# mLSTM keys laid out by token: transposing DMAs over halves of words in place of products with the identity

## The chip, the cores and the metric

The kernel runs on 1 core of one Trainium2 chip. The metric is device time in microseconds (us); the kernel before takes 910.33 us, the median of three runs (909.4 to 910.87). Lower is better.

## The reference, cut to what matters

One layer of a hybrid decoder on 1024 prompt tokens and on 8 single tokens with a saved state. One large input projection feeds two branches, a gated linear recurrence (RG-LRU) and an mLSTM with 4 heads of 256 features; the gated results of both go through an output projection and a norm. The change touches the mLSTM alone, which runs over chunks of 128 tokens:

```python
u = hn @ w_in                       # (1024 tokens) x (1024 -> 7168 + 8 columns)
xa, za, uq, uk, uv, uo, zb, ui, uf = split(u)
k = uk.reshape(B, S, H_B, DK) * DK ** -0.5

def mlstm_chunk(carry, inp):        # q, k, v: (B, L=128, H=4, 256)
    C, n, m = carry
    ...
    P = w * einsum('bthk,bshk->bhts', q, k)
    num = (einsum('bhts,bshv->bthv', P, v)
           + ginter[..., None] * einsum('bthk,bhkv->bthv', q, C))
    den = sum(P, -1) + ginter * einsum('bthk,bhk->bht', q, n)
    h = num / maximum(abs(den), exp(-m_t))
    C_new = carry_scale * C + einsum('bhs,bshk,bshv->bhkv', decay, k, v)
    n_new = carry_scale * n + einsum('bhs,bshk->bhk', decay, k)
    return (C_new, n_new, mL), h
```

(`ginter`, `carry_scale` and `decay` are broadcast as the letters say.) Two sums use the keys in two layouts. The scores (`P`) sum over the 256 features, so TensorE wants features on its partitions. The memory (`C_new`) sums over the 128 tokens, so there the keys are wanted with tokens on the partitions.

## The kernel before, in words

Everything runs on one core, in one program without loops at run time. The Tile framework's scheduler fixes the order of each engine's instructions; each engine and each DMA queue then works strictly in order. Loads (`ld`) stand in the queue of SyncE (SP), stores (`stq`) in that of GpSimd (POOL).

**Projections.** The input projection is done in 14 units of two column pairs each (`UNITS`, in the order `v0v1 x0y0 q0k0 x1y1 q1k1 x2y2 v2v3 q2k2 x3y3 q3k3 o0o1 o2o3 z0z1 z2z3`). A unit is 14 pieces: the seven products of a Strassen scheme, each for two halves. All large products are made of three: each operand is split into a high part and a low rest (`split`, L70 to L74: a cast on ScalarE, a subtraction on VectorE), and `mm3` (L64 to L68) multiplies high by high, high by low and low by high. A unit's weights come by two loads of L258 into `raw`. ScalarE and VectorE bring the results from PSUM into staging tiles (`stg`, made by `sg`, 2 KB per partition each); there are seven of them (`NSTG`), used in turn by all that asks for one. From a staging tile POOL's queue stores to scratch memory in DRAM: queries and keys of head h to `d_qk[h]` ([4, 128, 1024]: two blocks of query features, two of key features, features on partitions), values to `d_v[h]`, gates to others.

**Work in between.** After each piece `pop_bg` (L730) takes one step from each of three lists of small work: `bg`, `rgq` (the RG-LRU, with loads of `xs` and `zsr` at L764, L766 and L770 and its gates' weights at L798) and, at the pieces in `DEC`, `dcq` (the 8 single tokens). What is put on the list `late` runs one round later.

**The mLSTM.** There are 32 items, n = 4 x chunk + head. The first four run during the last unit (`m_first`), the other 28 in the final loop, where the products of the output projection (`fill`: `mm3` with `ps_o<-wo,mh`) are laid between their steps. For one item:

- `m_load(n)` loads queries and keys (`qk`, 128 x 4 x 128) and values (`vt`, 128 x 256), each into one of two buffers, two items ahead. `w_load` brings the row of decays `W`.
- `m_k(n)` makes the weights `We` (L1213), and splits queries and memory (`qh`/`ql`, `Ch`/`Cl`).
- `m_a(n)` makes, in one PSUM bank `s`, the scores (two products in full float32, which the profile counts as four instructions at L1232) and beside them the keys with tokens on partitions: `TE.transpose` of the two key blocks, products with the identity `idF` (L1234). ScalarE then makes the scaled keys `kh` from that bank (L1240), VectorE their rest `kl` (L1242) and the weighted scores `pf` (L1241); values and weighted scores are split (`vh`/`vl`, `ph`/`pl`).
- `m_b(n)` makes query times memory (`qp`, six products), which ScalarE scales (L1288), keys times values (`kv`, six), scores times values (`tr`, three), and updates the memory `Cf`.
- Later steps normalise (`so`, L1313), transpose the head's output (L1339) and split it into `mh`/`ml`, the operands of the output projection.

Of the kernel before, what the change touches and what calls it, by code (L numbers as in the profile page):

```python
# [9 lines left out]
F32 = mybir.dt.float32  # L10
F32R = mybir.dt.float32r
BF16 = mybir.dt.bfloat16
AF = mybir.ActivationFunctionType
ALU = mybir.AluOpType
PSUM = bass.MemoryType.PSUM
# [28 lines left out]
UNITS = "v0v1 x0y0 q0k0 x1y1 q1k1 x2y2 v2v3 q2k2 x3y3 q3k3 o0o1 o2o3 z0z1 z2z3".split()  # L44
NWS, NSTG, LEAD = 6, 7, 2
DEC = 4, 5, 7, 9, 11
RQ = [Q_P1, Q_P2, Q_P5, Q_P6, Q_P7, Q_P4, Q_P3]
NR, NZ = 28, 4

# [2 lines left out]
def hymba_kernel(  # L52
# [118 lines left out]
    d_gd = dram.tile([NB, 8], F32, name="d_gd")  # L171
    d_dv = [dram.tile([NB, 256], F32, name=f"d_dv{h}") for h in range(NH)]
    d_qk = [dram.tile([4, P, T], F32, name=f"d_qk{h}") for h in range(NH)]
    d_v = [dram.tile([T, 256], F32, name=f"d_v{h}") for h in range(NH)]
    d_so = [dram.tile([T, 256], F32, name=f"d_so{h}") for h in range(NH)]
    d_zs = dram.tile([KC, P, T], F32, name="d_zs")
# [226 lines left out]
    grow = [sg([1, HT], f"grow{half}") for half in range(2)]  # L403
    for half in range(2):
        A.dma_start(grow[half], g_norm[:, half * HT:(half + 1) * HT])
    warm = const([P, 1], "warm")
    A.activation(warm, ones[:, 0:1], AF.Sqrt)
    es_f = ExitStack()
    fp = es_f.enter_context(tc.tile_pool(name="f_start", bufs=1))
# [315 lines left out]
        V.tensor_scalar(em_t, em_t, 1e-15, None, op0=ALU.max)  # L725
        V.tensor_scalar(de_t, de_t, 1.0 / 16.0, None, op0=ALU.mult)

    bg, rgq, dcq = deque(), deque(), deque()

    def pop_bg(n=1, rg=1, dc=1):  # L730
        run_late()
        for q, m in ((bg, n), (rgq, rg), (dcq, dc)):
            for _ in range(m):
                if q:
                    q.popleft()()
# [216 lines left out]

    ds_ = {}

    def dec_rows(half):

        pvd = ps("s", [NB, 512])
        for m in range(4):
            TE.transpose(pvd[:, m * P:(m + 1) * P], dv[:, 4 * half + m, :], idF)
        vr = sg([NB, 512], "vr")  # L960
        V.tensor_copy(vr, pvd)
        for h in range(2):
            stq(d_dv[2 * half + h], vr[:, h * 256:(h + 1) * 256])
# [112 lines left out]
    def decode_outputs():  # L1076
# [45 lines left out]
            V.tensor_tensor(v4(nn, kb), v4(nq, kb), bh(dGI), op=ALU.mult)  # L1122
            V.tensor_tensor(v4(kwn, kb), v4(dk, kb), bh(dW), op=ALU.mult)
        V.tensor_tensor(nn, nn, kwn, op=ALU.add)
        nrow = mx["pn"].tile([64, 512], F32, tag="nrow", name="nrow")
        for half in range(2):
            g = slice(32 * half, 32 * half + NB)
            pn = ps("s", [NB, 512])
# [4 lines left out]

    es_m, es_n, es_t = ExitStack(), ExitStack(), ExitStack()
    mx = {}

    def m_open1():

        fpr["es"].close()
        mx["p"] = mp = es_m.enter_context(tc.tile_pool(name="f_m1", bufs=1, reuse_waits="tile"))
        mx["Cf"] = [mp.tile([P, 2, 258], F32, tag=f"Cf{h}", name=f"Cf{h}") for h in range(NH)]
        mx["v"] = vhl = [mp.tile([P, 258], F32R, tag=f"v{n}", name=f"v{n}") for n in "hl"]
        mx["pn"] = es_n.enter_context(tc.tile_pool(name="f_mn", bufs=1, reuse_waits="tile"))
        V.memset(vhl[0][:, 256:257].bitcast(F32), 1.0)
        V.memset(vhl[0][:, 257:258].bitcast(F32), 0.0)
        V.memset(vhl[1][:, 256:258].bitcast(F32), 0.0)
        w_load(0)
        m_load(0)  # L1150
        m_load(1)
        so_load(0)
        so_load(1)

    def m_open2():

        es_n.close()
        es_d.close()
        pt = es_t.enter_context(tc.tile_pool(name="f_mt", bufs=1, reuse_waits="tile"))
        w_fetch(0, 1, pt.tile([P, 4, HT], F32, tag="wc01", name="wc01"))  # L1160
        m_load(4)
        m_load(5)
# [9 lines left out]
    def m_load(n):  # L1172
        if n >= 4 * NCH:
            return
        c, h = n // 4, n % 4
        ts_ = slice(c * L, (c + 1) * L)
        w_load(n + 1)
        qk = mx["p"].tile([P, 4, L], F32, tag="qk", name="qk", bufs=2)
        ld(qk, d_qk[h][:, :, ts_].rearrange("m p t -> p m t"))
        vt = mx["p"].tile([P, 256], F32, tag="vt", name="vt", bufs=2)  # L1180
        ld(vt, d_v[h][ts_, :])
        it[n] = {"qk": qk, "vt": vt}

    Ws = {}

# [39 lines left out]
    def m_a(n):  # L1225
        c, h = n // 4, n % 4
        d = it[n]
        sk = ps("s", [P, 512])
        S, kn = sk[:, 0:128], sk[:, 256:512]
        qk = d["qk"]  # L1230
        for kb in range(2):
            TE.matmul(S, qk[:, 2 + kb, :], qk[:, kb, :], start=kb == 0, stop=kb == 1)  # L1232
        for kb in range(2):
            TE.transpose(kn[:, kb * P:(kb + 1) * P], qk[:, 2 + kb, :], idF)  # L1234
        pf = mx["p"].tile([P, L], F32, tag="pf", name="pf")
        ph = mx["p"].tile([P, L], F32R, tag="ph", name="ph")
        pl = mx["p"].tile([P, L], F32R, tag="pl", name="pl")
        kh = mx["p"].tile([P, 256], F32R, tag="kh", name="kh")
        kl = mx["p"].tile([P, 256], F32R, tag="kl", name="kl")
        A.mul(kh, kn, de_t[:, c, h:h + 1])  # L1240
        V.scalar_tensor_tensor(pf, S, 1.0 / 16.0, d["W"], op0=ALU.mult, op1=ALU.mult)  # L1241
        V.scalar_tensor_tensor(kl, kn, de_t[:, c, h:h + 1], kh.bitcast(F32), op0=ALU.mult, op1=ALU.subtract)  # L1242
        split(mx["v"][0][:, 0:256], mx["v"][1][:, 0:256], d["vt"])
        split(ph, pl, pf)
        d.update(ph=ph, pl=pl, kh=kh, kl=kl)

    def m_kv(n, tags):

# [310 lines left out]
            wo_split(m14=3, m15=12)  # L1559

    def fms():
        return mx["p2"].tile([P, 4], F32, tag="fms", name="fms", bufs=2)

    tails, stored = [], []

# [78 lines left out]
        stq(p_n[0, 0].rearrange("h (kb p) -> (h kb) p", p=P), rows)  # L1644

    def last_tile():
        ms = mx["p2"].tile([P, 6], F32, tag="ms7", name="ms7")
        y = [sg([P, HT], f"y{n}") for n in range(2)]
        yg = [sg([P, HT], f"yg{n}") for n in range(2)]
        for n in range(2):  # L1650
# [83 lines left out]
    for u in range(1, len(units)):  # L1734
        roles_on()
        for n, (q, s) in enumerate(PIECES):
            if n in PREP:
                preps(7 * (u - 1) + PREP.index(n) + 1 + LEAD)
            product(u, q, s)
            pop_bg(2 if u == 1 or u == last_u else 1, 1, part % 14 in DEC)  # L1740
            part += 1
            if u == last_u and n in DUE:
                wo_due(DUE.index(n))
            if n == 13:
                for kind, j in units[u]:
                    if kind == "x":
                        rg_unit(j)
                for half in range(2):
                    if u == max(unit_of["v", 2 * half], unit_of["v", 2 * half + 1], 1):
                        bg.append(lambda half=half: dec_rows(half))  # L1750
                for h in range(NH):
                    if done_h[h] == u:
                        bg.append(lambda h=h: decode_queue(h))
                if u == last_u - 1:
                    dgen = decode_outputs()

                    def step():
                        next(dgen, None)
                        run_late()
                    state["out"] = [step] * 5 + [m_open2]  # L1760
            if n % 2 and not state["m"] and u > max(done_h) and not (bg or rgq or dcq or late):
                m_start()
            if u == last_u and n == 1:
                if not state["m"]:
                    while bg or rgq or dcq or late:
                        pop_bg()
                    m_start()
                bg.extend(state["out"])
# [11 lines left out]
    for n in range(4, N):  # L1780
# [7 lines left out]
        if n == 6:  # L1788
            mx["gf"] = gf = [sg([P, HT], f"gf{m}") for m in range(2)]
            for m in range(2):  # L1790
                stq(gf[m], g_final[m * HT:(m + 1) * HT].partition_broadcast(P))
        m_load(n + 2)
        if h == 3 or n == 4:
            z_load(c if h == 3 else 0)
        if h == 0:
# [78 lines left out]
```

## Time and profile before

| | before |
|---|---|
| median of three runs | 910.33 us (909.4 to 910.87) |
| profiled execution, its own time | 909.62 us |
| its span in the profile | 907.8 us |
| ScalarE, DMA moved | busy 586.1 us (65%), 167.76 MB |
| HBM read, written | 108.00 MB, 62.92 MB |
| chain that ended last, largest lines | TensorE's `ps_o` L66 6%, L68 6%, L67 6%; `ps_s` L1232 1%; `ps_s` L1234 1% |

The profile is one execution. Busy time of an engine is the sum over its instructions; PE is TensorE's multiplying, PEld its loading of weights, which runs beside it; DVE is VectorE, ACT ScalarE, POOL GpSimd, and SPq the queue of loads. A row of the order of time has the start in the span (us), the duration (us), the engine, the line, the operation and the tiles, output left of `<-`, with buffer numbers left out. A row of the groups has the count after x, the busy time (us), the mean (ns), and the idle time of that engine just before with what ended it. A row of the waits has engine, tile and line of who waits, then for whom, then the summed wait, how many, and the longest.

### The profile page before, as it was taken

To read this page: it belongs to the slowest core of one execution; us is meant where nothing else is said; L and a number is where in the kernel's file an instruction comes from. 1 tells how busy PE (TensorE), PEld (TensorE's weight loads), DVE (VectorE), ACT (ScalarE), POOL (GpSimd) and SP (SyncE) were. 2 spreads that over 40 slices of the span, in tenths; PEclk is the share of its full clock that TensorE was granted. 3 is DMA by queue.
4 is the path that set the end of the run, shared out by engine and by line. 5 is a ranking of instruction groups with operands and counts; after the bars stand their busy time and mean duration, and the time that the engine had idled before them with its cause. 6 is when DMAs were issued, how large, how long until landed. Compare 5 with 4: busy or idle time off the path is not lost. (4 is left out here: it accounts for less than half of the span.)

```text
span 907.8 us, 16671 instructions
## 1 busy us (share of the span) xinstructions
PE 895.5 (99%) x5889; PEld 764.4 (84%) x5889; DVE 740.4 (82%) x1528; ACT 586.1 (65%) x1086; POOL 194.9 (21%) x322
## 2 busy tenths in 40 slices
PE   8999999999999999999999999999999999999996
PEld 6997778887888998888889998887788888888885
DVE  6974779869689978798999877679998779888973
ACT  7663446767667776576768775547787568556652
POOL 1111113012222222323333244010111111111120
PEclk9999999999999999999999999999999999999999
DMA  6412457347556557657585555536689889856531
GB/s 200 152 62 92 140 155 262 112 154 233 192 188 217 179 176 235 202 158 243 188 272 191 193 179 189 170 124 226 202 228 256 203 224 287 216 144 178 178 123 70
DMA packets 127037, 167.76 MB, mean 185 GB/s; under 512 B 17212, under 2 KB 94084, under 8 KB 126946
## 3 DMA queue, kind: packets, MB, share of 16 engines
q1 hardware_dynamic: 105334, 103.68, 37.1%
q0 software_dynamic: 21616, 63.02, 21.6%
q8 instruction: 46, 0.75, 0.4%
q14 instruction: 37, 0.30, 0.1%
q10 hardware_dynamic: 4, 0.00, 0.0%
HBM read 108.00 MB, written 62.92 MB: 188 GB/s over the span
## 5 line engine op out<-in xcount | busy, mean ns | idle before, releaser
L72 ACT CAST wh<-raw 128x1024 fp32r<-128x1024 f32 x91 | 95.4, 1049 | 72.8 <-DVE raw L299 21.2
L73 DVE TENSOR_TENSOR wl<-raw,wh 128x1024 fp32r<-128x1024 f32 x91 | 111.1, 1221 | 36.7 <-ACT wh L72 21.4
L66 PE MATMUL ps_X<-cb_hi,wh 128*128 128x512 f32 x320 | 126.6, 396 | 0.0
L68 PE MATMUL ps_X<-cb_hi,wl 128*128 128x512 f32 x320 | 125.4, 392 | 0.0
L67 PE MATMUL ps_X<-cb_lo,wh 128*128 128x512 f32 x320 | 125.1, 391 | 0.0
L66 PEld LDWEIGHTS ps_X<-cb_hi,wh 128*128 128x128 f32 x320 | 60.1, 188 | 15.9 <-issue 2.5
L68 PEld LDWEIGHTS ps_X<-cb_hi,wl 128*128 128x128 f32 x320 | 60.1, 188 | 13.3 <-issue 0.6
L67 PEld LDWEIGHTS ps_X<-cb_lo,wh 128*128 128x128 f32 x320 | 60.1, 188 | 12.8 <-issue 0.8
L66 PE MATMUL ps_Y<-cb_hi,wh 128*128 128x512 f32 x160 | 63.6, 398 | 0.3 <-DVE s L350 0.3
L68 PE MATMUL ps_Y<-cb_hi,wl 128*128 128x512 f32 x160 | 62.5, 391 | 0.0
L67 PE MATMUL ps_Y<-cb_lo,wh 128*128 128x512 f32 x160 | 62.5, 391 | 0.0
L66 PE MATMUL ps_X<-wh,cb_hi 128*128 128x256 f32 x192 | 54.8, 286 | 0.0
L67 PE MATMUL ps_X<-wl,cb_hi 128*128 128x256 f32 x192 | 54.4, 283 | 0.0
L68 PE MATMUL ps_X<-wh,cb_lo 128*128 128x256 f32 x192 | 54.4, 283 | 0.0
L66 PE MATMUL ps_o<-wo,mh 128*128 128x512 f32 (+1 forms) x136 | 53.1, 391 | 0.0
L68 PE MATMUL ps_o<-wo,ml 128*128 128x512 f32 (+1 forms) x136 | 51.6, 380 | 0.0
L67 PE MATMUL ps_o<-wo,mh 128*128 128x512 f32 (+1 forms) x136 | 51.5, 379 | 0.0
L66 PEld LDWEIGHTS ps_X<-wh,cb_hi 128*128 128x128 f32 x192 | 36.8, 191 | 1.5 <-ACT Z L279 0.4
L67 PEld LDWEIGHTS ps_X<-wl,cb_hi 128*128 128x128 f32 x192 | 36.8, 192 | 0.2
L68 PEld LDWEIGHTS ps_X<-wh,cb_lo 128*128 128x128 f32 x192 | 36.8, 192 | 0.0
L66 PEld LDWEIGHTS ps_Y<-cb_hi,wh 128*128 128x128 f32 x160 | 30.2, 188 | 6.9 <-DVE s L350 0.7
L68 PEld LDWEIGHTS ps_Y<-cb_hi,wl 128*128 128x128 f32 x160 | 30.0, 188 | 6.5
(573 smaller groups left out, 2746.9 us busy)
## 6 DMA issues: line engine op xcount, KB each, us to landing
raw<-in_w_in_dram SPq DMA_DIRECT2D x55, 512.0 KB
Cb<-in_state_mlstm_C_dram SPq DMA_DIRECT2D x32, 256.0 KB
out_dram<-Cb POOLq DMA_DIRECT2D x32, 256.0 KB, 5.0
qk<-d_qk SPq DMA_DIRECT2D x32, 256.0 KB
ring<-d_ro SPq DMA_DIRECT2D x26, 256.0 KB
d_qk<-s POOLq DMA_DIRECT2D x24, 256.0 KB, 4.4
d_x<-s POOLq DMA_DIRECT2D x16, 256.0 KB, 2.5
zsr<-d_y SPq DMA_DIRECT2D x16, 256.0 KB
```

Of the source, the lines that this page charges most:

```text
L66: TE.matmul(out, ah, bh, start=first, stop=False, skip_group_check=True)
L67: TE.matmul(out, ah, bl, start=False, stop=False, skip_group_check=True)
L68: TE.matmul(out, al, bh, start=False, stop=last, skip_group_check=True)
L72: a = A.copy(hi, src)
L73: V.tensor_tensor(lo, src, hi.bitcast(F32), op=ALU.subtract)
```

## The change

The keys by token no longer come from TensorE. During the projections, at pieces 2, 6 and 10 of the units that follow a unit with keys (`TURN`), a new list `ktq` gives one step of `k_turn(h, i)`, four for each head, 16 in all. Such a step takes a staging tile `tt` and issues one DMA on SP's queue that reads 256 tokens of the head's two key blocks from `d_qk`, takes each float32 for two halves of 16 bits, and writes them transposed: tokens' halves on the partitions, features along them. Two rounds later POOL's queue stores the tile to a new scratch array `d_kt[h]` (token, half, feature).

In the mLSTM, `k_load(n)` loads the item's values and the item's keys by token (`kt`, 128 x 2 x 256 halves), one item ahead, each into a single buffer (`vt` had two). `m_rows(n)` has ScalarE put the halves back next to each other (`A.copy` over the bits, which gives `kn` in float32). `m_a` makes only the scores in bank `s`; `kh` and `kl` read `kn`, and the weighted scores are written over `We` instead of into a tile `pf`. Room is made by taking `warm` and `nrow` from other tiles, and `fms`, now of eight columns, also serves the last tile. The product, the splits and everything behind them are as they were.

```diff
+TURN = 2, 6, 10
...
+    d_kt = [dram.tile([T, 2, 256], U16, name=f"d_kt{h}") for h in range(NH)]
...
-    warm = const([P, 1], "warm")
+    warm = sp2[:, 0:1]
...
-    bg, rgq, dcq = deque(), deque(), deque()
+    bg, rgq, dcq, ktq = deque(), deque(), deque(), deque()
-    def pop_bg(n=1, rg=1, dc=1):
+    def pop_bg(n=1, rg=1, dc=1, kt=1):
         run_late()
-        for q, m in ((bg, n), (rgq, rg), (dcq, dc)):
+        for q, m in ((bg, n), (rgq, rg), (dcq, dc), (ktq, kt)):
...
+    def k_turn(h, i):
+        def f():
+            tt = sg([P, 4, 256], "tt", U16)
+            nc.sync.dma_start_transpose(tt, d_qk[h][2:4, :, i * 256:(i + 1) * 256].bitcast(U16).rearrange("m p t -> (m p) t"))
+            rows = d_kt[h][i * 256:(i + 1) * 256].rearrange("t e c -> (t e) c").rearrange("(b p) c -> p b c", p=P)
+            late.append(lambda: late.append(lambda: stq(rows, tt)))
+        return f
...
-        nrow = mx["pn"].tile([64, 512], F32, tag="nrow", name="nrow")
+        nrow = sg([64, 512], "nrow")
...
-        vt = mx["p"].tile([P, 256], F32, tag="vt", name="vt", bufs=2)
-        ld(vt, d_v[h][ts_, :])
-        it[n] = {"qk": qk, "vt": vt}
+        it[n] = {"qk": qk}
+    def k_load(n):
+        if n < 4 * NCH:
+            c, h = n // 4, n % 4
+            vts[n] = mx["p"].tile([P, 256], F32, tag="vt", name="vt")
+            ld(vts[n], d_v[h][c * L:(c + 1) * L])
+            kts[n] = mx["p"].tile([P, 2, 256], U16, tag="kt", name="kt")
+            ld(kts[n], d_kt[h][c * L:(c + 1) * L])
+    def m_rows(n):
+        kn = mx["p"].tile([P, 256], F32, tag="kn", name="kn")
+        A.copy(kn.bitcast(U16).rearrange("t (c e) -> t e c", e=2), kts.pop(n))
+        return kn
...
     def m_a(n):
-        sk = ps("s", [P, 512])
-        S, kn = sk[:, 0:128], sk[:, 256:512]
+        S = ps("s", [P, L])
+        kn = m_rows(n)
         qk = d["qk"]
         for kb in range(2):
             TE.matmul(S, qk[:, 2 + kb, :], qk[:, kb, :], start=kb == 0, stop=kb == 1)
-        for kb in range(2):
-            TE.transpose(kn[:, kb * P:(kb + 1) * P], qk[:, 2 + kb, :], idF)
-        pf = mx["p"].tile([P, L], F32, tag="pf", name="pf")
+        pf = d["W"]
...
-        split(mx["v"][0][:, 0:256], mx["v"][1][:, 0:256], d["vt"])
+        split(mx["v"][0][:, 0:256], mx["v"][1][:, 0:256], vts.pop(n))
...
+        if n < NH:
+            k_load(n + 1)
...
-        return mx["p2"].tile([P, 4], F32, tag="fms", name="fms", bufs=2)
+        return mx["p2"].tile([P, 8], F32, tag="fms", name="fms", bufs=2)
...
-        ms = mx["p2"].tile([P, 6], F32, tag="ms7", name="ms7")
+        ms = fms()
...
-            pop_bg(2 if u == 1 or u == last_u else 1, 1, part % 14 in DEC)
+            pop_bg(2 if u == 1 or u == last_u else 1, 1, part % 14 in DEC, part % 14 in TURN)
...
+                    if kind == "k":
+                        ktq.extend(k_turn(j, i) for i in range(4))
...
         m_load(n + 2)
+        k_load(n + 1)
```

**TensorE, one item of the final loop.** The rows of the order are line, operation, output and inputs, shape, and a count where rows repeat. `ps_o` is a bank of the output projection, `wo` and `mh`/`ml` its operands, `ps_qp<-idF,hh` the transposition of a head's output, `ps_s` the bank of the scores. Before:

```order
L66 MATMUL ps_o<-wo_8474,mh_9563 128x512
L67 MATMUL ps_o<-wo_8474,mh_9563 128x512
L68 MATMUL ps_o<-wo_8474,ml_9564 128x512
L1339 MATMUL ps_qp<-idF,hh 128x128 x4
L1232 MATMUL ps_s<-qk 128x128 x2
L1234 MATMUL ps_s<-idF,qk 128x128 x2
L66 MATMUL ps_o<-wo_8556,mh_9563 128x512
L67 MATMUL ps_o<-wo_8556,mh_9563 128x512
L68 MATMUL ps_o<-wo_8556,ml_9564 128x512
```

After the change (L68 to L70 are the former L66 to L68, L1257 is the former L1232):

```order
L68 MATMUL ps_o<-wo_8537,mh_9636 128x512
L69 MATMUL ps_o<-wo_8537,mh_9636 128x512
L70 MATMUL ps_o<-wo_8537,ml_9637 128x512
L1257 MATMUL ps_s<-qk 128x128 x2
L68 MATMUL ps_o<-wo_8620,mh_9636 128x512
L69 MATMUL ps_o<-wo_8620,mh_9636 128x512
L70 MATMUL ps_o<-wo_8620,ml_9637 128x512
```

The scores are followed by a product of the output projection; the two rows' worth of products with `idF` and `qk` is gone. The four transpositions of the head's output (L1339) stand elsewhere in this item's order.

**ScalarE, one item of the final loop**, from the split of its queries (`qh`) on; `kh` are the scaled keys, `kn` and `kt` the new tiles. Before:

```order
L72 CAST qh<-qk 128x256
L72 CAST Ch<-Cf_6149 128x516
L1627 ACTIVATE ps_o,fms<-y_9250 128x512
L1288 ACTIVATE hh<-ps_qp,gi_t 128x257
L72 CAST vh<-vt 128x256
L1240 ACTIVATE kh<-ps_s,de_t 128x256
L1313 ACTIVATE so,ms<-hh 128x256
L72 CAST ph<-pf 128x128
```

After (L74 is the former L72, L1652 the former L1627, L1313 the former L1288, L1263 the former L1240, L1338 the former L1313, L1238 the former L1213):

```order
L74 CAST qh<-qk 128x256
L74 CAST Ch<-Cf_6200 128x516
L1652 ACTIVATE ps_o,fms<-y_9320 128x512
L1313 ACTIVATE hh<-ps_qp,gi_t 128x257
L1263 ACTIVATE kh<-kn,de_t 128x256
L74 CAST vh<-vt 128x256
L1206 COPY kn<-kt 128x2x256
L74 CAST ph<-We 128x128
L1338 ACTIVATE so,ms<-hh 128x256
L1238 ACTIVATE We<-We 128x128
```

The copy L1206 is new, between the split of the values and that of the weighted scores. `kh` moved ahead of the split of the values and reads `kn` in place of the bank `ps_s`; the weighted scores are split from `We`.

**SP's queue at the second transposition**, in the unit that follows the first head's keys; `raw` are the next unit's weights, `zsr` and `xs` the RG-LRU's operands, `Cb` a saved state of the single tokens. Before:

```order
L798 DMA graw_1400<-in_w_igate_dram 64x2x64 x2
L770 DMA zsr<-d_y_147 128x512
L764 DMA xs<-d_x_140 128x512
L258 DMA raw_4_2137<-in_w_in_dram 128x4x256 x2
L766 DMA xs<-d_x_140 128x515
L989 DMA Cb<-in_state_mlstm_C_dram 128x2x256 x4
```

After (L773, L767, L261 and L769 are the former L770, L764, L258 and L766):

```order
L773 DMA zsr<-d_y_151 128x512
L962 DMA_TRANSPOSE tt<-d_qk_125 128x4x256
L767 DMA xs<-d_x_144 128x512
L261 DMA raw_4_2145<-in_w_in_dram 128x4x256 x2
L962 DMA_TRANSPOSE tt<-d_qk_125 128x4x256
L769 DMA xs<-d_x_144 128x515
L1001 DMA Cb<-in_state_mlstm_C_dram 128x2x256 x4
```

The second and third transposing DMA stand ahead of, and between, the loads that were there; each waits in SP's order for a free staging tile.

**POOL's queue at the same place** after the change; `d_kt<-tt` is the new store, `d_p` and `d_x` are other results of the projections (L390 is the former L387):

```order
L888 DMA d_ro_158<-rm 128x2x128
L889 DMA d_p_167<-in_x_prompt_dram 128x512
L891 DMA d_r_165<-rm 128x256
L964 DMA d_kt_129<-tt 128x4x256
L390 DMA d_x_144<-s_2112 128x512
L390 DMA d_y_152<-s_2034 128x512
```

The new store stands between the stores of other results and goes when its transposition has landed.

More of the change, by code (lines that the diff above doesn't have):

```diff
@@ L12 @@
 BF16 = mybir.dt.bfloat16
+U16 = mybir.dt.uint16
 AF = mybir.ActivationFunctionType
@@ L1132, in decode_outputs @@
             stq(s_n[0].rearrange("b h k -> b (h k)")[:, half * 512:(half + 1) * 512], nrow[g])
-    es_m, es_n, es_t = ExitStack(), ExitStack(), ExitStack()
+    es_m, es_t = ExitStack(), ExitStack()
     mx = {}
@@ L1144, in m_open1 @@
         mx["v"] = vhl = [mp.tile([P, 258], F32R, tag=f"v{n}", name=f"v{n}") for n in "hl"]
-        mx["pn"] = es_n.enter_context(tc.tile_pool(name="f_mn", bufs=1, reuse_waits="tile"))
         V.memset(vhl[0][:, 256:257].bitcast(F32), 1.0)
@@ L1150, in m_open1 @@
         m_load(0)
+        k_load(0)
         m_load(1)
@@ L1155, in m_open2 @@
     def m_open2():
-        es_n.close()
         es_d.close()
@@ L1179, in m_load @@
         ld(qk, d_qk[h][:, :, ts_].rearrange("m p t -> p m t"))
-        vt = mx["p"].tile([P, 256], F32, tag="vt", name="vt", bufs=2)
-        ld(vt, d_v[h][ts_, :])
-        it[n] = {"qk": qk, "vt": vt}
+        it[n] = {"qk": qk}
+    kts, vts = {}, {}
+    def k_load(n):
[9 more added lines that the diff above has]
+        return kn
     Ws = {}
@@ L1760, in hymba_kernel @@
                     state["out"] = [step] * 5 + [m_open2]
-            if n % 2 and not state["m"] and u > max(done_h) and not (bg or rgq or dcq or late):
+            if n % 2 and not state["m"] and u > max(done_h) and not (bg or rgq or dcq or ktq or late):
                 m_start()
@@ L1764, in hymba_kernel @@
                 if not state["m"]:
-                    while bg or rgq or dcq or late:
+                    while bg or rgq or dcq or ktq or late:
                         pop_bg()
```

## The prediction

> **What bounds the kernel now.** I read the page first, then busy time by stretches, then the waits of TensorE, and last its order of time around one head of one chunk.
>
> ```profile
> PE 895.5 (99%) x5889; PEld 764.4 (84%) x5889; DVE 740.4 (82%) x1528; ACT 586.1 (65%) x1086; POOL 194.9 (21%) x322
> ```
>
> ```profile
> 100.00:200.00 100.00, 99.34 (x550) 80.14 (x549) 81.90 (x171) 60.29 (x93) 19.95 (x37) 1.00 0.53 176
> 200.00:300.00 100.00, 100.00 (x676) 82.49 (x675) 86.85 (x146) 71.82 (x105) 23.63 (x39) 1.00 0.61 198
> 600.00:640.00 40.00, 39.65 (x254) 29.66 (x253) 36.33 (x78) 24.73 (x39) 4.27 (x9) 1.00 0.56 184
> 640.00:700.00 60.00, 59.28 (x317) 50.47 (x316) 56.00 (x121) 47.34 (x103) 10.04 (x16) 1.00 0.79 231
> 750.00:800.00 50.00, 50.00 (x297) 40.93 (x296) 44.62 (x113) 36.56 (x90) 7.03 (x11) 1.00 0.85 240
> 880.00:908.00 28.00, 20.46 (x117) 17.39 (x115) 12.23 (x28) 7.64 (x22) 2.74 (x5) 0.93 0.20 76
> ```
>
> The columns are start and end, length, then busy time of PE, PEld, DVE, ACT and POOL, the granted clock, the busy share of the DMA engines and GB/s. TensorE does not stand still between 200 and 300 us nor between 750 and 800, and the clock is granted in full. It stands still for 7.5 us only in the last 28, behind the last tile. Of its waits elsewhere one belongs to this change:
>
> ```profile
> PE ps_s L1339 <- DVE kl L1242: 0.6, 1, 0.6
> ```
>
> So a nanosecond of TensorE's own time that goes ahead of 880 us should move the end by as much, as long as no other engine falls behind. VectorE is the next one: 56.0 of 60 us between 640 and 700.
>
> **What is removed.** 64 products with the identity, two for each of 32 heads of chunks. Their busy time overlaps that of their neighbours, so I go by starts.
>
> ```profile
> 812.76 0.39 PE L68 MATMUL ps_o<-wo,ml 128*128 128x512 f32 x1
> 813.00 0.60 PE L1232 MATMUL ps_s<-qk 128*128 128x128 f32 x4
> 813.44 0.38 PE L1234 MATMUL ps_s<-idF,qk 128*128 128x128 f32 x2
> 813.57 0.48 PE L66 MATMUL ps_o<-wo,mh 128*128 128x512 f32 x1
> 813.89 0.39 PE L67 MATMUL ps_o<-wo,mh 128*128 128x512 f32 x1
> ```
>
> ```profile
> 662.79 0.61 PE L1232 MATMUL ps_s<-qk 128*128 128x128 f32 x4
> 663.15 0.37 PE L68 MATMUL ps_tr<-vh,pl 128*128 128x258 f32 x1
> 663.36 0.38 PE L1234 MATMUL ps_s<-idF,qk 128*128 128x128 f32 x2
> ```
>
> In the first fence, which is the usual case, the scores (L1232) start at 813.00 and the next ordinary product at 813.57: 0.57 us. In the second the order happened to put an ordinary product directly behind the scores, as the change does everywhere: it starts 0.36 us after them. The pair therefore costs 0.57 - 0.36 = 0.21 us. The slow step into the next product stays either way (0.32 us from L66 to L67 where 0.23 is usual; 0.21 from L68 to the products in the second fence, though it has only 258 columns). 32 x 0.21 = **6.7 us**. The low end is the distance from the pair's own start to its successor, 0.13 us, or 4.2 us in all. I take 0.21, because the second fence shows the very sequence that is left.
>
> The 0.6 us wait above also goes: it was for the bank of the scores, which VectorE held until it had read the keys from it. They no longer lie there.
>
> **What is added, and what hides it.** On ScalarE one copy for each item, 512 halves of words per partition.
>
> ```profile
> L72 ACT CAST vh<-vt 128x256 fp32r<-128x256 f32 x32 | 12.7, 397 | 0.1
> L1503 ACT COPY r<-ps_o 128x512 f32<-128x512 f32 x16 | 9.3, 580 | 8.5 <-PE ps_o L68 8.5
> ```
>
> ```profile
> ACT kh L1240 <- PE ps_s L1234: 10.6, 9, 1.6
> ```
>
> ```profile
> 640.00:700.00 60.00, 2.29 (x12) 1.49 (x12) 1.00 0.79 231
> ```
>
> Between 397 ns (256 elements) and 580 ns (512); I take 580, the same count of elements, so 32 x 0.58 = 18.6 us. The last row counts L1234 alone: 12 products, so six items, fall in 640 to 700, or 3.5 us of copies against 60 - 47.3 = 12.7 us in which ScalarE does nothing; between 750 and 800 it is as much against 13.4. ScalarE also loses 10.6 us of waiting for the identity's products. The new order puts the scaled keys of the next item directly behind the scaling of the product with the memory (L1288), ahead of the next scores, so they are early. On the path this costs nothing on average. Where VectorE is nearly full (640 to 700) I let half of the six items' gain, 0.6 us, be lost to it.
>
> The tile of values is loaded into one buffer where there were two. Its load may now go only when its low part has been read:
>
> ```profile
> 844.00 0.40 DVE L73 TENSOR_TENSOR vl<-vt,vh 128x256 fp32r<-128x256 f32 x1
> 847.84 0.39 ACT L72 CAST vh<-vt 128x256 fp32r<-128x256 f32 x1
> 852.35 0.28 PE L66 MATMUL ps_kv<-vh,kh 128*128 128x258 f32 x1
> ```
>
> From 844.40 ScalarE would wait for a load that takes over 3.4 us, and TensorE only for one that takes over 852.35 - 844.40 - 0.39 = 7.6 us. Loads on SP have no landing time in the profile; the nearest bound is a late one:
>
> ```profile
> 233.77 0.94 SPq L258 DMA_DIRECT2D raw<-in_w_in_dram  x2
> 241.73 1.05 ACT L72 CAST wh<-raw 128x1024 fp32r<-128x1024 f32 x1 [3.81 <-DMA raw<-in_w_in_dram]
> ```
>
> Two loads of 512 KB took up to 8.0 us to be there. One of 128 KB should need about half or less; behind the cast stand the other splits of the same item, which have the same slack. I take nothing, with 28 x (8.0 - 7.6) = 11 us as the far end. That wait of 3.8 us also shows that a late weight tile cost TensorE nothing there (100.00 of 100.00 us): its operands are split two products ahead.
>
> The 16 transposing DMAs stand in SP's queue, their 16 stores in POOL's, all during the projections. Around the second of them:
>
> ```profile
> 181.09 0.34 SPq L770 DMA_DIRECT2D zsr<-d_y  x1
> 181.53 0.38 SPq L764 DMA_DIRECT2D xs<-d_x  x1
> 187.28 1.86 SPq L258 DMA_DIRECT2D raw<-in_w_in_dram  x2
> ```
>
> ```profile
> 182.62 0.56 POOL L888 DMA_DIRECT2D d_r<-rm  x1
> 188.87 0.55 POOL L387 DMA_DIRECT2D d_x<-s  x1 [5.69 <-DVE s L364]
> ```
>
> SP issues it after the first of these rows, at 181.4; the weights behind it were only asked for at 187.28, when their buffer came free, so an issue of up to 5 us is hidden. POOL stores its result ahead of the row at 188.87, before which it had waited 5.7 us. So the transposition may take 188.9 - 181.4 = 7.5 us before POOL's next store is late. How long one takes, no row shows. As a plain transfer it would take
>
> ```profile
> q1 hardware_dynamic: 105334, 103.68, 37.1%
> d_qk<-c POOLq DMA_DIRECT2D x8, 256.0 KB, 3.3
> ```
>
> 0.371 x 907.8 / 103.68 = 3.25 us of all engines per MB, so 0.85 us for 256 KB (0.262 MB), and 3.3 us until it lands if it behaves as that store. I take 3.3; the upper end is open and is the rival below. Transposes, their stores and the loads of their result add 12.6 MB; at that price 41 us of DMA time, spread over 750 us. The engines' share rises from 0.85 to about 0.90 between 750 and 800 (six loads of 128 KB, each 0.43 us, in 50 us), which can delay loads but not fill the engines.
>
> The page "VectorE: DVE Perf Modes" of the Trainium skill (The three transpose paths) speaks against the change: a 128x128 transpose of two-byte elements takes 390 ns on TensorE and 1309 ns by DMA, and TensorE is to be used where its destination serves. The row here has the pair at 0.21 us, cheaper still, but on the engine that is full. Each DMA here holds eight such tiles, an estimate from that page of 10.5 us if they go one after the other. The page "DMA: Bandwidth & Descriptors" (Latency and other measured facts) has 261 GB/s, an estimate of 1.0 us. By the second the sum stays as it is; by the first it stays too, with 0.9 us left below the point at which the slow rival, further down, begins.
>
> **The sum.** 6.7 + 0.6 - 0.6 = 6.7 us off the profiled execution's 909.62 us (its span is 907.8), so 902.9. The median shown is 910.33, 0.71 above, so **903.6 us**. From both ends of the terms: at most 6.7 + 0.6, with the 0.7 us that TensorE waits between 640 and 700 and the 0.66 + 0.35 us of the two other stretches gone as well, gives 901.3; at least 4.2 - 1.3 (all six tight items lost) gives 907.4.
>
> **Rivals.**
>
> *The freed time is waited away: no change, 908.5 to 912.2, chance 0.12.* TensorE would wait 0.21 us per item for ScalarE or VectorE. For it: VectorE at 44.6 of 50 us gets 48.7 us for the same work, and ScalarE has one more step ahead of each item. Against: the copy hangs on a load and not on TensorE, and ScalarE's waits for the products go.
>
> *The transposition is slow: slower, chance 0.12.* It holds one of the seven staging tiles from its issue until its store has landed. How long a tile's turn is:
>
> ```profile
> 177.54 1.11 SPq L258 DMA_DIRECT2D raw<-in_w_in_dram  x2
> 219.88 1.04 SPq L258 DMA_DIRECT2D raw<-in_w_in_dram  x2
> ```
>
> ```profile
> d_qk<-s POOLq DMA_DIRECT2D x24, 256.0 KB, 4.4
> ```
>
> The first weights of one unit and of the next are asked for 42.3 us apart. The unit that follows the first head's keys takes 18 staging tiles with three of the new ones, so a tile's turn comes after 7 x 42.3 / 18 = 16.4 us. The store takes 0.56 us of issue (as L387 above) and 4.4 to land. So from 16.4 - 5.0 = 11.4 us on per DMA the next result of a product has no tile, ScalarE's copy waits in order, the banks stay full and TensorE stops. At 13 us it is 16 x 1.6 = 26 us: 903.6 + 26 = 929. Against it: 13 us is fifteen times the plain transfer's engine time. For it: elements of two bytes are no shape that any row here has. The estimate of 10.5 us from the Trainium skill's page "VectorE: DVE Perf Modes" lies just inside.
>
> *The change doesn't do what it says* only if the products with the identity had been hidden behind the weight loads: then 910. The two fences of starts speak against it; it is part of the first rival's chance.
>
> **How the numbers follow.** A measurement of this kernel can tell about 0.2%, 1.8 us, from no change. The forecast with its own ends, 901.3 to 907.4, has 0.68; 0.04 lies between 907.4 and 908.5, and 0.04 below 901.3. So faster 0.76, same 0.12, slower 0.12. The range from 901.3 to 910.0 takes in the forecast, the gap and two thirds of the first rival: 0.68 + 0.04 + 0.08 = 0.80.
>
> **What would show it.** No line for the identity's products, scores followed by an ordinary product after about 0.36 us, and TensorE's sum of busy time lower by at least 6 us. Copies near 0.58 us that no one on TensorE waits for. DMA transposes that land in under 7 us; POOL waiting for them, or evacuations waiting for a store of theirs, would mean the slow rival. TensorE waiting for the head products' operands would mean the single buffer or VectorE. The prediction is wrong if TensorE's idle time ahead of 880 us grows by more than 2 us.

## The result, and the profile after

| | before | after |
|---|---|---|
| median (lowest to highest), 6 runs each | 910.58 us (909.4 to 912.18) | 933.62 us (927.59 to 935.74) |
| ratio, 95% interval | | 1.0236 (1.0209 to 1.0264) |
| profiled execution, its span | 909.62, 907.8 us | 934.3, 932.5 us |

The change makes the kernel 23 us slower. The forecast was 903.6 us, faster, and the result lies outside its range, near 929, the price of the rival that the transposition is slow, which it gave a chance of 0.12.

The page of the changed kernel, first row (the lines of code are 2 to 25 higher than before: L66 to L68 are now L68 to L70):

```profile
PE 899.3 (96%) x5825; PEld 763.8 (82%) x5825; DVE 739.5 (79%) x1528; ACT 601.7 (65%) x1116; POOL 207.2 (22%) x338
```

TensorE has 64 products fewer and is busy 3.8 us longer, because its clock was lower at times (granted 0.989 on average, 0.998 before); and it stands still for 932.5 - 899.3 = 33.2 us, where it was 12.3. Where, the stretches show (start and end, length, busy time of PE, PEld, DVE, ACT, POOL, granted clock, share of DMA, GB/s). After:

```profile
200.00:300.00 100.00, 100.00 (x674) 82.44 (x673) 84.27 (x143) 69.58 (x102) 26.55 (x44) 1.00 0.75 224
400.00:460.00 60.00, 54.09 (x303) 43.20 (x304) 47.11 (x87) 39.13 (x57) 20.08 (x31) 1.00 0.76 220
500.00:520.00 20.00, 16.08 (x118) 15.68 (x117) 12.37 (x20) 11.08 (x19) 7.92 (x12) 0.91 0.83 245
640.00:700.00 60.00, 56.60 (x288) 44.29 (x287) 54.41 (x101) 44.65 (x85) 9.75 (x16) 0.97 0.67 193
750.00:800.00 50.00, 47.18 (x254) 40.45 (x253) 40.59 (x95) 35.00 (x78) 8.18 (x11) 0.97 0.87 252
```

Before, two stretches that the prediction did not show:

```profile
400.00:460.00 60.00, 60.00 (x334) 48.87 (x333) 52.31 (x90) 42.35 (x62) 18.57 (x29) 1.00 0.69 226
500.00:520.00 20.00, 20.00 (x221) 19.06 (x221) 16.11 (x21) 15.57 (x23) 3.73 (x6) 1.00 0.64 215
```

Up to 300 us, with eight transpositions asked for (the last at 297.41), nothing is lost. Then there are two large losses: one in the projections (400 to 520), one in the final loop (from 680). TensorE's waits of the changed kernel, largest four:

```profile
PE ps_X L68 <- ACT s L360: 3.9, 1, 3.9
PE ps_kv L68 <- ACT vh L74: 3.8, 2, 2.7
PE ps_D L68 <- DVE dqk L289: 3.2, 1, 3.2
PE ps_tr L1552 <- DVE hh L1320: 2.6, 1, 2.6
```

A finer measure, used below as **lag**: both programs have the same 4272 products of `mm3`, so the start of the n-th in one trace is compared with the n-th in the other. In the change the lag is 0.4 us where before is at 305 us, 1.9 at 320, 8.9 at 459, 14.5 from 513 to 565, 13.2 at 655, and then climbs in four steps of about 4 us to 27.3 at 786; it ends at 25.1 (the times are those of the kernel before). Between the steps it falls by about 0.2 us for each item: the gain is there.

**The loss in the projections, first place.** Order of time on SP, POOL and ScalarE after the change:

```profile
422.54 1.27 SPq L962 DMA_TRANSPOSE tt<-d_qk  x1
430.29 0.76 POOL L964 DMA_DIRECT2D d_kt<-tt  x1 [6.83 <-DMA tt<-d_qk]
431.04 1.08 POOL L390 DMA_DIRECT2D d_y<-c  x2
433.91 0.34 SPq L773 DMA_DIRECT2D zsr<-d_y  x1
434.35 1.92 SPq L1001 DMA_DIRECT2D Cb<-in_state_mlstm_C_dram  x4
437.53 0.72 ACT L1028 ACTIVATE Cb<-Cb,dGI 128x512 f32<-128x512 f32 x1 [8.20 <-DMA Cb<-in_state_mlstm_C_dram]
```

POOL waits 6.8 us in order for the transposition; the store of `d_y` behind it goes late; SP's load of `zsr` needs that store, and the loads of `Cb` stand behind `zsr`; ScalarE waits 8.2 us for `Cb`, with results of products queued behind. The lag grows by 6.0 us here (8.9 - 2.9). In the kernel before, SP waits for the landing of that store, too, so the store has no slack; its wait was

```profile
SPq L770 <- DMA d_y<-c: 11.2, 1, 11.2
```

**Second place.** The order around 505 us, and TensorE behind it:

```profile
504.72 0.72 POOL L888 DMA_DIRECT2D d_ro<-rm  x1 [9.11 <-DVE rm L887]
504.98 1.26 SPq L962 DMA_TRANSPOSE tt<-d_qk  x1
510.43 0.59 ACT L360 COPY s<-ps_X 128x512 f32<-128x512 f32 x1 [4.91 <-DMA d_ro<-rm]
511.07 0.39 PE L68 MATMUL ps_X<-wh,cb_hi 128*128 128x256 f32 x1 [3.92 <-ACT s L360]
```

ScalarE cannot copy a result: the staging tile whose turn it is still holds `rm`, whose store POOL issued late. POOL waits there for the RG-LRU in the kernel before, too:

```profile
494.60 0.72 POOL L885 DMA_DIRECT2D d_ro<-rm  x1 [10.10 <-DVE rm L884]
```

Before, ScalarE had no wait of this kind there. The seven tiles outlasted those 10 us; with one more taker in their turn they don't.

**The loss in the loop.** Load, cast, and the products that wait for it:

```profile
681.89 0.32 SPq L1199 DMA_DIRECT2D vt<-d_v  x1
689.22 0.40 ACT L74 CAST vh<-vt 128x256 fp32r<-128x256 f32 x1 [3.81 <-DMA vt<-d_v]
689.67 0.71 PE L68 MATMUL ps_kv<-vh,kh 128*128 128x258 f32 x2 [2.71 <-ACT vh L74]
690.18 0.63 PE L70 MATMUL ps_o<-wr5h,ro 128*128 128x512 f32 x1
690.61 0.63 PE L68 MATMUL ps_o<-wr5h,ro 128*128 128x512 f32 x1
```

Before, the load of the same kind at about the same time, and the cast that reads it (the casts follow the loads in order; one at 687.84 us still reads the load before this one):

```profile
682.94 0.98 SPq L1181 DMA_DIRECT2D vt<-d_v  x1
696.17 0.39 ACT L72 CAST vh<-vt 128x256 fp32r<-128x256 f32 x1
```

With two buffers the load had 13.2 us; with one it has the 3.5 us until ScalarE wants it (689.22 - 3.81 - 681.89), and this one took 7.3. The halves are waited for as much; ScalarE's waits from 640 us on, after:

```profile
ACT vh L74 <- DMA vt<-d_v: 9.1, 6, 3.8
ACT kn L1206 <- DMA kt<-d_kt: 8.8, 3, 4.9
```

### The profile page after: what moved, and what is told of

It is laid out like the page before. It is cut to its first block, busy times and chain, and to the rows that moved or that the text cites. A ratio compares the mean times of both kernels' runs of the same rounds, so it can differ in the third digit from the quotient of the medians.

```text
span 932.5 us, 16722 instructions
## 1 busy us (share of the span) xinstructions
PE 899.3 (96%) x5825; PEld 763.8 (82%) x5825; DVE 739.5 (79%) x1528; ACT 601.7 (65%) x1116; POOL 207.2 (22%) x338
## 5 line engine op out<-in xcount | busy, mean ns | idle before, releaser
L74 ACT CAST wh<-raw 128x1024 fp32r<-128x1024 f32 x91 | 95.4, 1049 | 77.3 <-DVE raw L302 21.7
L68 PE MATMUL ps_X<-cb_hi,wh 128*128 128x512 f32 x320 | 126.7, 396 | 0.0
L70 PE MATMUL ps_X<-cb_hi,wl 128*128 128x512 f32 x320 | 125.4, 392 | 0.0
L68 PEld LDWEIGHTS ps_X<-cb_hi,wh 128*128 128x128 f32 x320 | 60.1, 188 | 16.7 <-issue 3.5
L70 PEld LDWEIGHTS ps_X<-cb_hi,wl 128*128 128x128 f32 x320 | 60.1, 188 | 13.4 <-issue 0.6
L68 PE MATMUL ps_Y<-cb_hi,wh 128*128 128x512 f32 x160 | 63.7, 398 | 1.0 <-DVE s L353 1.0
L70 PE MATMUL ps_Y<-cb_hi,wl 128*128 128x512 f32 x160 | 62.6, 391 | 0.0
L68 PE MATMUL ps_X<-wh,cb_hi 128*128 128x256 f32 x192 | 55.5, 289 | 3.9 <-ACT s L360 3.9
L70 PE MATMUL ps_X<-wh,cb_lo 128*128 128x256 f32 x192 | 55.0, 287 | 0.0
L68 PE MATMUL ps_o<-wo,mh 128*128 128x512 f32 (+1 forms) x136 | 53.2, 391 | 0.0
L70 PE MATMUL ps_o<-wo,ml 128*128 128x512 f32 (+1 forms) x136 | 51.8, 381 | 0.0
L68 PEld LDWEIGHTS ps_X<-wh,cb_hi 128*128 128x128 f32 x192 | 37.3, 194 | 5.7 <-ACT s L360 4.1
L70 PEld LDWEIGHTS ps_X<-wh,cb_lo 128*128 128x128 f32 x192 | 37.5, 195 | 0.0
L68 PEld LDWEIGHTS ps_Y<-cb_hi,wh 128*128 128x128 f32 x160 | 30.1, 188 | 8.1 <-DVE s L353 1.9
L1206 ACT COPY kn<-kt 128x512 uint16<-128x512 uint16 x32 | 24.8, 774 | 16.8 <-DMA kt<-d_kt 12.9
```

The source lines that it names most:

```text
L68: TE.matmul(out, ah, bh, start=first, stop=False, skip_group_check=True)
L70: TE.matmul(out, al, bh, start=False, stop=last, skip_group_check=True)
L74: a = A.copy(hi, src)
L1206: A.copy(kn.bitcast(U16).rearrange("t (c e) -> t e c", e=2), kts.pop(n))
```

## The experiments

The runs stand in the order of the questions: where the loss is, then what makes it in the projections, then in the loop. The baseline of each was 910.0 to 910.5 us. Unless a run says otherwise, its ratio's interval is clear of 1.

### The two losses apart

**e1_proj_only**: the change, with the loop's old way of making keys and two buffers of values.

```diff
-            vts[n] = mx["p"].tile([P, 256], F32, tag="vt", name="vt")
+            vts[n] = mx["p"].tile([P, 256], F32, tag="vt", name="vt", bufs=2)
...
-            ld(kts[n], d_kt[h][c * L:(c + 1) * L])
...
+        for kb in range(2):
+            TE.transpose(kn[:, kb * P:(kb + 1) * P], qk[:, 2 + kb, :], idF)
```

> The 16 transposing DMAs and their 16 stores run during the projections as in the change; the head loop has its products with the identity and two buffers of values back, and nothing reads the stored keys. Theory: in the profile of the change TensorE fell 14.5 us behind the kernel before between 300 and 530 us, ahead of the loop, because POOL's and SP's queues stand in order behind late transpositions; so 910.6 + 14.5 = 925 us, with the same lag at the same places (438, 507 us). Rival: the projections lose only together with the loop's loads, or the DMAs are hidden, as predicted: 910 to 912 us.

923.79 us, 13.8 over before; lag 12.7 at 513 us, at the same places, and nearly flat in the loop (13.4 at its end). As the theory had it: the DMAs and their stores alone cost this.

**e2_loop_only**: the loop of the change, no transpositions.

```diff
-            ld(kts[n], d_kt[h][c * L:(c + 1) * L])
+            ld(kts[n], d_one[c * L:(c + 1) * L])
...
-                        ktq.extend(k_turn(j, i) for i in range(4))
+                        pass
```

> The head loop is that of the change; the 16 transpositions and their stores are left out, and the halves of the keys are loaded from an array of ones in DRAM that is filled at the start, so the keys by token, and with them memory and results, are not the reference's. Theory: the loop by itself gains 32 x 0.21 = 6.7 us and loses about 17 us in four or five stalls on the single buffers of values and halves: 910.6 + 17 - 6.5 = 921 us. Rival: those stalls came from the shift in time that the projections brought (other DMAs met the loads): 904 us.

918.28 us, 8.3 over before, of which 2.2 are the filling of the array of ones (lag at 223 us). So the loop by itself loses 6 us net. The two losses add up to 19.8 of the 23.0 us. In the change the loop has four steps of about 4 us, here only one of that size (5.1, at 680 us) and smaller ones; why the change has more was not followed. Neither theory (921) nor rival (904) alone: the loop loses without the shift in time, and more with it.

### In the projections

**e4_plain_dma**: `ld(tt, ...)` of the same 256 KB in place of `dma_start_transpose`.

> The change with a plain load of the same 256 KB in place of each transposing DMA, the same tile, queue and store; the loop's halves of keys come from an array of ones, so the keys by token are left out. Theory: the loss of the projections comes from waiting in order for a staging tile and for the landing, and a plain load waits as well: the lag of 14.5 us ahead of the loop shrinks by less than half, 927 to 934 us. Rival: the transposing itself is what is slow: the lag ahead of the loop falls to under 3 us, about 921 us.

927.08 us, at the lower end of the theory's range. Less the filling of the ones (1.4 us), the lag at 513 us is 9.6 instead of 14.5: the step near 438 us is down from 6.0 to 1.9, the one at 505 stays (6.3). So what the transposing adds to a plain load makes most of the first; the second needs no transposing.

**e7_no_store** and **e8_slot_only**, both from e1:

```diff
-            late.append(lambda: late.append(lambda: stq(rows, tt)))
```

and, for e8, also

```diff
-            nc.sync.dma_start_transpose(tt, d_qk[h][2:4, :, i * 256:(i + 1) * 256].bitcast(U16).rearrange("m p t -> (m p) t"))
+            ld(tt[:, 0, 0:64], x_prompt[0, 0:P, 0:32].bitcast(U16))
```

> As the first run of this study (transpositions in the projections, nothing reads them, the loop as before, 923.8 us), without the 16 stores of their result; a tile comes free when the transposition has landed. Theory: the stall at 438 to 455 us (5.6 us) comes from POOL, whose next stores wait in order for the transposition, and goes; that at 505 us (6 us) comes from the turn of the staging tiles and stays or halves: 915 to 919 us. Rival (the transpositions' own DMA time or SP's queue): 922 to 925 us.

> As the run before, with a load of 128 bytes per partition into the tile in place of each transposing DMA: it takes a staging tile at the same places in SP's order and gives it back soon. Theory: the turn of the staging tiles is what makes the stall at 505 us, so about 6 us of lag stays and the rest goes: 914 to 918 us. Rival (it is the transfer's duration and the store, not the turn): 910 to 911 us.

918.89 and 912.34 us. ScalarE at the second place, in e7 and then in e8:

```profile
505.75 0.58 ACT L360 COPY s<-ps_X 128x512 f32<-128x512 f32 x1 [7.17 <-DMA tt<-d_qk]
```

```profile
499.82 0.58 ACT L360 COPY s<-ps_X 128x512 f32<-128x512 f32 x1 [2.96 <-DMA tt<-in_x_prompt_dram]
```

The copy waits for the staging tile that the transposition holds: 7.2 us; and 3.0 us even when all that `tt` holds is a load of 16 KB. So of 13.5 us (923.79 less 910.31, these runs' baseline), 2.0 (912.34 - 910.31) are the turn of the tiles alone, 6.6 (918.89 - 912.34) what the transposing DMA adds to it, its duration in a tile and its traffic together, and 4.9 (923.79 - 918.89) the stores in POOL's order. In e7 the lag at 459 us is 2.4 instead of 6.7, as the theory had it, but the second step grew from 6.0 to 7.2; the turn alone was priced too high, at 6, and e8 lies between its theory and its rival.

**e9_spread**: `TURN = 4, 11` in place of `2, 6, 10`.

> As the first run of this study (923.8 us), with two transpositions in each unit of the projections, at pieces 4 and 11, in place of three at pieces 2, 6 and 10. Theory: a transposition costs only where POOL's, SP's and the tiles' turns meet a late one (438 and 505 us), so other places change the loss by several us: 912 to 919 us. Rival: each costs the same wherever it stands (13.4 / 16 = 0.84 us): 922 to 925 us.

924.95 us: not better than e1, and in the rival's range. But the rival's equal price per DMA isn't it either: the lag comes in few places, much the same as in e1, in other portions (2.4 us at 317, 2.7 around 450, 7.3 between 480 and 505, 3.1 in the loop). Which stores and tiles were late there was not followed.

### In the loop

**e5_loop_two_vt**: no transpositions, no loads of halves, two buffers of values. **e6_loop_one_vt**: the same with one.

```diff
-            vts[n] = mx["p"].tile([P, 256], F32, tag="vt", name="vt")
+            vts[n] = mx["p"].tile([P, 256], F32, tag="vt", name="vt", bufs=2)
...
-        A.copy(kn.bitcast(U16).rearrange("t (c e) -> t e c", e=2), kts.pop(n))
+        A.copy(kn.bitcast(U16).rearrange("t (c e) -> t e c", e=2), it[n]["qk"][:, 2:4, :].rearrange("p m t -> p (m t)").bitcast(U16).rearrange("t (c e) -> t e c", e=2))
```

(The first two lines are e5's alone.)

> The loop of the change with two buffers of values, without the loads of halves: the copy on ScalarE takes the keys' halves from the tile of queries and keys (same count, same strides on its output), and transpositions and stores in the projections are left out; so the keys by token, and with them memory and results, are not the reference's. Theory: the two terms of the prediction's sum are right and what is left out here is all that cost time: 910.0 - 6.7 = 903.3 us, 902 to 905. Rival: the copy on ScalarE, or the weighted scores written over the weights, costs time in the loop too: 906 to 910 us.

> As the run before, with one buffer of values as in the change; the same part is left out. Theory: the single buffer of values alone brings stalls where the DMA engines are full (around 685, 705 and 770 us): 908 to 913 us. Rival: it needs the loads of halves beside it to be late: 903 to 905 us.

904.60 us (0.994, 0.9923 to 0.9957) and 907.54 us (0.9968, 0.9956 to 0.9979). The first is the forecast without its hidden costs: 5.7 us gained of the 6.7 counted. The single buffer alone takes half of that back.

**e13_halves_alone**: the load goes to the halves' single buffer, no values are loaded. **e12_unread_halves**: e6 with an extra load that nothing reads.

> The same traffic as the loop with one buffer of values (907.5 us): the load of 128 KB goes into a single buffer that the copy on ScalarE reads, as in the change, and no values are loaded; their split reads the tile of queries and keys, so values and keys are not the reference's. Theory: one single buffer costs about 3 us whichever it is, and the two together more than their sum: 906 to 910 us. Rival: the halves' buffer is the costly one, since the copy stands ahead of more of ScalarE's work: 912 to 916 us.

> As the loop with one buffer of values and no loads of halves (907.5 us), with a load of 128 KB for each item into a single buffer at the place of the halves' load, which nothing reads: its traffic and its place in SP's queue without a wait on it. Keys by token are left out as there. Theory: what the change lost in the loop beyond that run is ScalarE's wait, in order, for the halves: 907 to 911 us. Rival: the extra 4.2 MB through DMA engines that are full anyway make values, weights and rings late: 914 to 918 us.

910.10 us (0.9986 to 1.0013) and 918.54 us. The first lies 0.1 us above its theory's range: this single buffer costs 5.5 us against e5, that of the values 2.9, so it does matter which it is, though less than the rival had it. The second is half a microsecond above the rival's range, but its trace shows another thing:

```profile
665.95 7.30 SPq L1201 DMA_DIRECT2D kt<-d_v  x2
678.72 0.62 ACT L74 CAST ro<-ring 128x512 fp32r<-128x512 f32 x1 [5.97 <-DMA ring<-d_ro]
```

Two unread loads into one buffer stood back to back and held SP's queue for 7.3 us; the loads of `ring` behind them came late. Its whole loss lies ahead of 690 us (lag 10.8 there, then falling to 6.4). So it does not tell, and two more runs were made.

**e14_two_keys** and **e15_two_values**: all the traffic, one of the two loads in two buffers.

> The loop with all the traffic of the change: values in one buffer, and a second load of 128 KB for each item into two buffers, which the scaling of the keys reads at once, without the copy on ScalarE (24.8 us of it are left out). Keys by token come from values, so memory and results are not the reference's. Theory: with one of the two loads in two buffers the loop loses as with one buffer of values alone, about 3 us against the 904.6 us without single buffers: 906 to 910 us. Rival: the extra traffic is what makes loads late: 914 to 918 us.

> As the run before with two buffers of values and one of the second load, which now comes free only after the rest of the keys is made; the same parts are left out. Theory: 906 to 910 us, as there. Rival (traffic): 914 to 918 us.

912.21 and 911.35 us (0.9994 to 1.0024): between the theory's range and the rival's. The same item in both, load, cast, product; e14, values in one buffer:

```profile
667.82 0.71 SPq L1199 DMA_DIRECT2D vt<-d_v  x1
675.23 0.40 ACT L74 CAST vh<-vt 128x256 fp32r<-128x256 f32 x1 [3.77 <-DMA vt<-d_v]
675.68 0.80 PE L68 MATMUL ps_kv<-vh,kh 128*128 128x258 f32 x2 [2.86 <-ACT vh L74]
```

e15, keys in one buffer:

```profile
668.08 0.32 SPq L1201 DMA_DIRECT2D kt<-d_v  x1
675.65 0.51 ACT L1262 ACTIVATE kh<-kt,de_t 128x256 fp32r<-128x256 f32 x1 [3.53 <-DMA kt<-d_v]
676.21 0.51 PE L68 MATMUL ps_kv<-vh,kh 128*128 128x258 f32 x2 [2.71 <-ACT kh L1262]
```

Whichever load has one buffer is the one that is waited for, 3.8 and 3.5 us, in the stretch where a load takes 7.5 us to land; the one with two buffers is in time. The second load adds 4.7 us to e6 (912.21 - 907.54, although e14 has no copy), most likely by way of that buffer: ScalarE's waits for `vt` add up to 9.3 us in e14 and to 4.8 in e6. As far as this shows, the traffic counts where a single buffer makes an engine wait for it. Adding the second single buffer and the copy gives e2's 916 (918.28 - 2.2).

**e3_two_buffers**: the change, with values in staging tiles and two buffers of halves.

> The change with values loaded into the rotating staging tiles and two buffers of halves of keys, nothing else. Theory: the loop's stalls on these loads go (about 17 us), the lag of the projections stays: 910.6 + 14.5 - 6.5 = 919 us. Rival (a full set of DMA engines makes any load late, one buffer or two): 930 to 934 us.

928.32 us: 5 of the expected 15 us. The waits on halves are gone, but a staging tile comes free late:

```profile
ACT vh L74 <- DMA vt<-d_v: 13.4, 8, 3.6
```

### Versions that might have been faster

**e10_two_heads**: transpositions and halves for heads 0 and 1 alone, values in two buffers, halves in staging tiles. **e11_late_heads**: all heads, those of 2 and 3 transposed in the second last unit.

> The change for heads 0 and 1 alone; heads 2 and 3 keep their products with the identity. Values have two buffers again, halves are loaded into the rotating staging tiles. Theory: the first eight transpositions cost 1.5 us at most (the lag of the first run of this study at 320 us), and the loop gains half of the 5.7 us that the loop with two buffers of values gained: 910.3 - 2.9 + 0 to 1.5 = 907.4 to 909 us. Rival: waits for staging tiles and loads of halves in the loop take it back: 911 to 915 us.

> The change for all heads, with the eight transpositions of heads 2 and 3 moved into the second last unit of the projections (after 530 us), values in two buffers, halves in the rotating staging tiles. Theory: there no RG-LRU loads or stores stand behind them in the queues, so the projections lose under 3 us, and the loop gains 5.7 us less what the extra loads of halves cost (up to 5 us): 906 to 912 us. Rival: eight transpositions in 40 us hold the staging tiles and the loop loses as in the change: 915 us and more.

928.45 and 939.18 us: e10 far above both of its ranges, e11 in its rival's. The projections lose less, though in e10 the first eight transpositions cost 4.3 us at 320 us and not 1.5: the lag is 5.2 us at 565 us in e10 and 1.35 in e11, and in e11 still 1.5 at 595, when seven of the eight late ones had been asked for, so late transpositions do find room. The loop takes it back, in e11 from its first items on, which start later. ScalarE's wait for halves, in e10 and e11:

```profile
ACT kn L1207 <- DMA kt<-d_kt: 17.2, 7, 6.0
```

```profile
ACT kn L1209 <- DMA kt<-d_kt: 21.4, 12, 4.9
```

A load into a staging tile can go only when the turn has come round, and had as little lead as with one buffer. A version with two buffers of its own for each of the two loads was not tried; nor was one with more staging tiles.

## Why the prediction was wrong, point by point

- **The products: right.** Scores and the next ordinary product, after:

```profile
675.82 0.61 PE L1257 MATMUL ps_s<-qk 128*128 128x128 f32 x4
676.18 0.48 PE L68 MATMUL ps_o<-wr3h,ro 128*128 128x512 f32 x1
```

  0.36 us, as taken, so 0.21 per item. e5 gained 5.7 of the 6.7 us; between 655 and 758 us its lag did not fall at all. For VectorE, half of six items, 0.6 us, had been allowed; in e5 it was busy for 24.9 of the first 25 us there and 62.7 of the other 78, so that VectorE alone held the gain back is not shown.
- **The copy: cheap, as said, though longer.** 774 ns instead of 580; e5 has it in full and is faster.

```profile
L1206 ACT COPY kn<-kt 128x512 uint16<-128x512 uint16 x32 | 24.8, 774 | 16.8 <-DMA kt<-d_kt 12.9
```

- **The single buffer of values: the first step that failed.** "One of 128 KB should need about half or less" of 8.0 us, "I take nothing". Loads took 7.3 us and more where the engines are full, and the cover was the wrong one: TensorE's 7.6 us do not help when ScalarE waits in order from 3.4 us on, with the next item's steps behind it. Alone it costs 2.9 us (e6).
- **The single buffer of halves: not costed at all.** The prediction spoke of the loads' share of the DMA engines and not of their lead. Alone it costs 5.5 us (e13). Both buffers together turn the loop's gain of 5.7 into a loss of 6 (e2), 11.7 us.
- **The transpositions: the second step that failed.** The sum took 3.3 us until one lands, and nothing for the delay. In the change POOL waited for eight of the 16, and those waits ended 3.9 to 8.6 us after the DMA was asked for; the longest:

```profile
395.54 1.44 SPq L962 DMA_TRANSPOSE tt<-d_qk  x1
404.18 0.75 POOL L964 DMA_DIRECT2D d_kt<-tt  x1 [3.52 <-DMA tt<-d_qk]
```

  "Around the second of them" there were 7.5 us of room; it took 7.1 (181.99 to 189.08), and nothing was lost. But that room was measured at one of 16 places, and it isn't the same at the others: near 430 us SP already waits for POOL's next store, near 505 POOL already waits for the RG-LRU. The term put at nothing is 13.8 us (e1).
- **The slow rival: right in its mechanism, wrong in its point and by luck near the result.** "The next result of a product has no tile, ScalarE's copy waits in order, the banks stay full and TensorE stops" is what e7 and e8 show at 505 us. It was to begin at 11.4 us per DMA, from an even turn of 16.4 us; POOL's 10.1 us of waiting for `rm`, visible before, had eaten most of that turn. Its 929 is close, but 11.7 us of the loss are the loop's, which this rival doesn't have. The estimate of 10.5 us per DMA from the Trainium skill's page "VectorE: DVE Perf Modes" (The three transpose paths) is above all eight of the change, 8.6 us at most; in e9 the longest took up to 10.9.

- **Two smaller things.** The prediction would be wrong, it said, if TensorE's idle time ahead of 880 us grew by more than 2 us: it went from 5.0 to 26.2 us. And the low end, 901.3, counts 0.6 us twice: the wait for `kl` stands at 668.53 us, inside the 0.7 us between 640 and 700; without that it is 901.9.

So 903.6 became 933.6 by 13.8 us in the projections and 11.7 in the loop, 1.0 less gain, and some 3.5 that appear only when both come together, whose division stays open.

## What to carry to other kernels

A load's price is not its duration but its lead: before a buffer is taken away, compare what is left between its release and its use with the slowest landing in the fullest stretch, on the engine that meets it first, which waits in order. A step added to shared queues and rotating tiles has to be followed at each place that it goes to, above all where the profile of before already has an engine waiting ten microseconds for nothing that matters. And an engine that is off the critical path stays off it only as long as what queues behind its waits can wait too.

## What was not expected of the hardware

A stall of TensorE costs more than its length. After the gap that ends at 689.67 (2.7 us idle, 3.1 from start to start), the products start 0.43 us apart (690.18 to 690.61) where 0.23 is usual, and the granted clock is halved for 3.4 us, which is not so after the gap of 3.2 us that ends at 442.32:

```profile
442.40:445.80 3.40, 2.90 (x12) 2.06 (x12) 3.25 (x6) 3.38 (x6) 0.99 (x1) 1.00 0.32 92
689.80:693.20 3.40, 3.40 (x13) 3.01 (x14) 2.07 (x6) 2.25 (x5) 0.20 (x1) 0.50 0.53 186
680.00:690.00 10.00, 6.70 (x37) 5.35 (x38) 8.12 (x22) 5.61 (x15) 2.60 (x5) 0.99 0.99 290
690.00:700.00 10.00, 10.00 (x48) 8.63 (x48) 7.02 (x20) 7.23 (x19) 1.75 (x2) 0.84 0.65 141
```

At 0.84 of the clock 10 us do the work of 8.4, so 1.6 us more are lost: half as much again as the stall. The change has five such stretches (from 512.3, 689.8, 717.1, 778.5 and 809.3 us), one in each of the loop's four steps; the kernel before has none ahead of 903 us. The Trainium skill's page "TensorE: Matmul & The Clock Gate" (The HAM clock gate) has the clock halved after an idle window of about 3.4 us. The halved clock is here, but the trace does not agree on the window: 2.7 us of idling were enough at 689.67, and 3.2 us did not do it at 442.32.

A transposing DMA occupies the DMA engines about twice as long as a plain one of its size, by the time that its packets take. The queue of loads in e1, e2 and e4:

```profile
q1 hardware_dynamic: 122230, 107.87, 39.8%
```

```profile
q1 hardware_dynamic: 109942, 107.87, 38.7%
```

```profile
q1 hardware_dynamic: 114294, 112.07, 39.7%
```

With the spans (920.8, 914.4 and 924.9 us; before 37.1% of 907.8) that is (366.5 - 336.8) / 16 = 1.9 us of all engines for each transposition, and (367.2 - 353.9) / 16 = 0.8 us for each plain load.
